# Label logits by masked sums on VectorE in place of 63 of 64 gathers, a tapered last group and one activation table set, in a softmax cross-entropy kernel

## The chip, the cores and the metric

The kernel runs on one core of one Trainium2 chip. The metric is device time in microseconds (us) of one execution. The profile's own span of an execution is 1.3 to 2 us shorter than the time reported for it, so differences inside a run are told in span, and verdicts in time.

Engines: ScalarE (ACT) computes the exponentials, VectorE (DVE) small reductions, GpSimd (POOL) issues the gathers, SyncE (SP) issues the loads, and 16 DMA engines move the data between HBM, the main memory, and SBUF, the on-chip memory. PSUM is a second on-chip memory. A load "lands" when all its data has arrived. `L85` is line 85 of the kernel in question, so the same statement has other line numbers in other kernels.

## The reference

```python
logits: float32 [16, 512, 32000]      # 8192 rows, 1.05 GB
labels: int32   [16, 512]
lse  = log(sum(exp(logits - max))) + max          # per row
loss = lse - logits[row, label[row]]              # float32 [16, 512]
```

Every logit must be read once. That is 1048.6 MB. The kernels leave out the maximum; with the drawn inputs this stays within tolerance.

## The kernel before

The 8192 rows stand as 128 partitions times G = 64 groups. A group has V = 32000 columns.

```python
idx[p, g] = (p * G + g) * V + label[p, g]         # GpSimd: iota, add
for g in range(G):                                # 64 gathers, 128 elements of 4 bytes each
    nc.gpsimd.indirect_dma_start(out=lab_logit[:, g:g + 1], in_=lg,
        in_offset=bass.IndirectOffsetOnAxis(ap=idx[:, g:g + 1], axis=1), ...)
...
for g in range(G):
    if g >= G - FINE_GROUPS:                      # last 3 groups: 8 tiles of 4000 columns each, 5 buffers
        for c in range(CF):
            tf = fine_pool.tile([P, WF], FP32)
            nc.sync.dma_start(out=tf[:], in_=lg_pg[:, g, c * WF:(c + 1) * WF])
            nc.scalar.activation(out=tf[:], in_=tf[:], func=Exp, accum_out=stats_col(g, c))
    else:                                         # 61 groups: 2 tiles of 16000 columns each, 2 buffers
        for c in range(C):
            t = data_pool.tile([P, W], FP32)
            nc.sync.dma_start(out=t[:], in_=lg_pg[:, g, c * W:(c + 1) * W])
            nc.scalar.activation(out=t[:], in_=t[:], func=Exp, accum_out=stats_col(g, c))
...
def finalize(lo, hi):   # sum of the stats (VectorE), Ln (ScalarE), subtract (VectorE), store
    ...
finalize(0, G - 1)
finalize(G - 1, G)
```

The exp is in place: only its row sum (`accum_out`) is of use. One buffer is free again when its exp is over.

The softmax here doesn't subtract the row's maximum and nothing guards it: scores larger than these inputs give would overflow.

## Time and profile before

| | before |
|---|---|
| time, median of 4 runs | 2440.01 us (2439.93 to 2440.22) |
| span of the profiled run | 2438.7 us |
| a 16000-column tile (8.19 MB) lands every | 18.90 us undisturbed, about 19.3 us while the gathers run |
| exp of a 16000-column tile | 13.54 us |
| last logits land | 2430.76 us |
| from there to the end | 7.9 us |

Lines of the page of the kernel before follow. First come the busy time of each engine, then the share of DMA busy time and the GB/s in 40 equal slices of the span. Then come the queue that fetches instructions (packets, MB, share), two groups of instructions (busy us, mean ns, idle time before them and who ended it), and the issues of the large loads (KB each, us from issue to landing).

```profile
span 2438.7 us, 851 instructions
...
DVE 1.7 (0%) x5; ACT 1754.4 (72%) x298; POOL 61.2 (3%) x70
...
DMA  9999999999999999999999999999999999999998
GB/s 404 437 420 422 435 437 435 429 429 437 437 436 428 431 435 437 435 432 428 435 436 436 435 427 434 436 437 435 427 432 436 437 435 425 434 437 432 426 430 360
...
q14 instruction: 6, 0.05, 0.0%
...
L85 ACT ACTIVATE t<-t 128x16000 f32<-128x16000 f32 x122 | 1651.4, 13536 | 642.9 <-DMA t<-in_logits_dram 642.9
...
L57 POOL DMA_INDIRECT lab_logit<-in_logits_dram,idx x64 | 60.5, 945 | 186.8 <-DMA lab_logit<-in_logits_dram,idx 184.2
...
t<-in_logits_dram SPq DMA_DIRECT2D x122, 8000.0 KB, 24.1
```

The load stream bounds this kernel. ScalarE is busy 72% of the time and had 642.9 us of idle time that ended with a landing. The DMA engines are above 90% in nearly every slice. 8.192 MB every 18.90 us is 433 GB/s.

The end of the timeline of the same kernel follows (start us, duration us, engine, line, operation, idle time before it and who ended it).

```profile
2430.84 3.54 ACT L76 ACTIVATE tf<-tf 128x4000 f32<-128x4000 f32 x1 [1.11 <-DMA tf<-in_logits_dram]
...
2434.49 1.28 ACT L101 ACT_TABLE_LOAD   x1
2434.50 0.16 DVE L96 TENSOR_REDUCE totals<-stats_last 128x1 f32<-128x8 f32 x1 [36.37 <-ACT tf L76]
2435.78 0.20 ACT L101 ACTIVATE logsum<-totals 128x1 f32<-128x1 f32 x1
2436.02 0.16 DVE L105 TENSOR_TENSOR res<-logsum,lab_logit 128x1 f32<-128x1 f32 x1 [1.35 <-ACT logsum L101]
2436.21 0.34 ACTq L109 DMA_DIRECT2D out_dram<-res  x1
```

The last of the 4000-column pieces has just landed at 2430.76. Then come an exp of 3.54 us, a table load of 1.28 us (in this trace one stands wherever ScalarE goes from Exp to Ln, at 2396.32 and 2434.49, and from Ln back to Exp, at 2398.62), Ln, subtract and store.

### The profile page before, as it was taken

The page shows a single profiled execution, that of the slowest core. Times are in us where ns is not written, and L with a number is a line of the kernel's source. Part 1 is how long each engine was busy: PE and PEld are TensorE (multiplying, and loading weights), DVE is VectorE, ACT ScalarE, POOL GpSimd, SP SyncE. Part 2 cuts the span into 40 slices and gives each one's busy share as a digit, 9 for nine tenths or more (in the row PEclk, how much of TensorE's full clock was granted, in tenths as well). Part 3 has the DMA queues.
Part 4 walks back from the last instruction along what each step waited for, and adds up shares of the span by engine and source line. Part 5 has one row for each costly group of instructions (what it writes and reads, how often), then busy time and mean ns, then how long its engine had stood idle before and what let it go on. Part 6 is the DMA issues. An engine that isn't in the chain of part 4 may idle for free.

```text
span 2438.7 us, 851 instructions
## 1 busy us (share of the span) xinstructions
DVE 1.7 (0%) x5; ACT 1754.4 (72%) x298; POOL 61.2 (3%) x70
## 2 busy tenths in 40 slices
DVE  0000000000000000000000000000000000000000
ACT  4777766777677767777677767777677767777697
POOL 3222000000000000000000000000000000000000
DMA  9999999999999999999999999999999999999998
GB/s 404 437 420 422 435 437 435 429 429 437 437 436 428 431 435 437 435 432 428 435 436 436 435 427 434 436 437 435 427 432 436 437 435 425 434 437 432 426 430 360
DMA packets 23510, 1048.77 MB, mean 430 GB/s; under 512 B 4688, under 2 KB 4816, under 8 KB 4816
## 3 DMA queue, kind: packets, MB, share of 16 engines
q1 hardware_dynamic: 21168, 1048.65, 99.6%
q0 software_dynamic: 2048, 0.04, 0.1%
q10 hardware_dynamic: 288, 0.03, 0.0%
q14 instruction: 6, 0.05, 0.0%
HBM read 1048.67 MB, written 0.03 MB: 430 GB/s over the span
## 4 chain that ended last, share of the span: by engine, by line
DMA 63%; ACT 36%; issue 0%; ACTq 0%; SPq 0%; DVE 0%
DMA t<-in_logits_dram 61%; ACT t L85 34%; DMA tf<-in_logits_dram 2%; ACT tf L76 2%; ACT L101 0%; ACT L76 0%; ACTq L85 0%; ACT logsum L101 0%; SPq L84 0%; DVE res L105 0%; SPq L48 0%; ACTq L109 0%; ACTq L76 0%
## 5 line engine op out<-in xcount | busy, mean ns | idle before, releaser
L85 ACT ACTIVATE t<-t 128x16000 f32<-128x16000 f32 x122 | 1651.4, 13536 | 642.9 <-DMA t<-in_logits_dram 642.9
L76 ACT ACTIVATE tf<-tf 128x4000 f32<-128x4000 f32 x24 | 84.7, 3530 | 14.6 <-DMA tf<-in_logits_dram 14.6
L57 POOL DMA_INDIRECT lab_logit<-in_logits_dram,idx x64 | 60.5, 945 | 186.8 <-DMA lab_logit<-in_logits_dram,idx 184.2
L85 ACT ACTIVATION_READ_ACCUMULATOR t<-t 128x1 f32 x122 | 22.7, 186 | 0.0
L85 ACT ACT_TABLE_LOAD x1 | 1.3, 1283 | 23.3 <-DMA t<-in_logits_dram 23.3
L76 ACT ACTIVATION_READ_ACCUMULATOR tf<-tf 128x1 f32 x24 | 4.5, 187 | 0.0
L101 ACT ACT_TABLE_LOAD x2 | 2.6, 1283 | 0.0
L96 DVE TENSOR_REDUCE totals<-stats 128x63 f32<-128x504 f32 x1 | 0.7, 678 | 2394.9 <-ACT tf L76 2394.9
L76 ACT ACT_TABLE_LOAD x1 | 1.3, 1283 | 0.8 <-DVE res L105 0.8
L66 DVE MEMSET stats<- 128x504 f32 x1 | 0.5, 478 | 0.9 <-PEq L127 0.9
L101 ACT ACTIVATE logsum<-totals 128x63 f32<-128x63 f32 (+1 forms) x2 | 0.5, 229 | 0.0
L105 DVE TENSOR_TENSOR res<-logsum,lab_logit 128x63 f32<-128x63 f32 (+1 forms) x2 | 0.4, 192 | 2.2 <-ACT logsum L101 2.2
L53 POOL TENSOR_TENSOR idx<-idx,labs 128x64 int32<-128x64 int32 x1 | 0.3, 318 | 1.8 <-DMA labs<-in_labels_dram 1.8
L96 DVE TENSOR_REDUCE totals<-stats_last 128x1 f32<-128x8 f32 x1 | 0.2, 161 | 36.4 <-ACT tf L76 36.4
L51 POOL IOTA idx<- 128x64 int32 x1 | 0.2, 172 | 0.4 <-PEq L138 0.4
L127 POOL MEMSET const-uint8-127<- 128x1 uint8 x1 | 0.1, 118 | 0.0
L127 POOL MEMSET const-bfloat16-1.0<- 128x1 bf16 x1 | 0.1, 113 | 0.0
L127 POOL MEMSET const-float32-0.0<- 128x1 f32 x1 | 0.1, 98 | 0.2 <-issue 0.2
L127 POOL MEMSET const-float32-1.0<- 128x1 f32 x1 | 0.1, 104 | 0.0
## 6 DMA issues: line engine op xcount, KB each, us to landing
t<-in_logits_dram SPq DMA_DIRECT2D x122, 8000.0 KB, 24.1
tf<-in_logits_dram SPq DMA_DIRECT2D x24, 2000.0 KB, 20.1
lab_logit<-in_logits_dram,idx POOLq DMA_INDIRECT x64, 33.4
labs<-in_labels_dram SPq DMA_DIRECT2D x1, 64.0 KB, 1.9
out_dram<-res ACTq DMA_DIRECT2D x1, 31.5 KB, 9.1
out_dram<-res ACTq DMA_DIRECT2D x1, 0.5 KB, 1.4
```

What stands on the lines that cost most here:

```text
L51: nc.gpsimd.iota(idx[:], pattern=[[V, G]], base=0, channel_multiplier=G * V)
L53: nc.gpsimd.tensor_tensor(out=idx[:], in0=idx[:], in1=labs32, op=mybir.AluOpType.add)
L57: nc.gpsimd.indirect_dma_start(out=lab_logit[:, g:g + 1], out_offset=None, in_=lg, in_offset=bass.IndirectOffsetOnAxis(ap=idx[:, g:g + 1], ...
L66: nc.vector.memset(stats[:], 0.0)
L76: nc.scalar.activation(out=tf[:], in_=tf[:], func=mybir.ActivationFunctionType.Exp, accum_out=stats_col(g, c),)
L85: nc.scalar.activation(out=t[:], in_=t[:], func=mybir.ActivationFunctionType.Exp, accum_out=stats_col(g, c),)
L96: nc.vector.reduce_sum(out=totals[:, lo:hi], in_=stats[:, lo:hi, :] if hi <= G - 1 else stats_last[:], axis=mybir.AxisListType.X,)
L101: nc.scalar.activation(out=logsum[:, lo:hi], in_=totals[:, lo:hi], func=mybir.ActivationFunctionType.Ln,)
L105: nc.vector.tensor_tensor(out=res[:, lo:hi], in0=logsum[:, lo:hi], in1=lab_logit[:, lo:hi], op=mybir.AluOpType.subtract,)
L127: nc = _bacc.Bacc("TRN2", target_bir_lowering=False, num_devices=1)
```

## The change

The intent is to take the 64 gathers off the DMA engines, by reading the label logits out of the tiles that are in SBUF anyway, and to shorten the end. For each quarter tile of 4000 columns one VectorE instruction computes `(column == label) * logit` and its row sum, which is the label's logit or 0. Only the last group still uses a gather. Now there are three buffers of 16000 columns. The last group comes in seven shrinking pieces. One table set that holds Exp and Ln is loaded once, at the start (the only table load in the trace of the changed kernel: 1.28 us, from 1.18 us on).

```diff
-    data_pool = ctx.enter_context(tc.tile_pool(name="data", bufs=2))
-    fine_pool = ctx.enter_context(tc.tile_pool(name="fine", bufs=5))
+    data = ctx.enter_context(tc.tile_pool(name="data", bufs=3))
+    masked = psum.tile([P, H], FP32)                            # H = 4000, never read
+    TAPER = [11200, 8000, 5600, 3500, 2000, 1100, 600]
...
-    nc.sync.dma_start(out=labs64[:], in_=labels_pg)
+    nc.scalar.dma_start(out=labs64[:], in_=labels_pg)
+    nc.scalar.preload_act_table_set("natural_log_exp_and_others")
...
-    for g in range(G):
-        nc.gpsimd.indirect_dma_start(out=lab_logit[:, g:g + 1], ...)
+    nc.gpsimd.indirect_dma_start(out=lab_logit[:, G - 1:G], ...)   # last group alone
...
+    for g in range(G - 1):
+        for c in range(C):
+            t = data.tile([P, W], FP32, tag="t")
+            nc.sync.dma_start(out=t[:], in_=lg_pg[:, g, c * W:(c + 1) * W])
+            for i in range(W // H):
+                h = c * (W // H) + i
+                nc.vector.scalar_tensor_tensor(
+                    out=masked[:], in0=cols[:], scalar=lab_at[:, h, g:g + 1],
+                    in1=t[:, i * H:(i + 1) * H],
+                    op0=ALU.is_equal, op1=ALU.mult,
+                    accum_out=found[:, g, h:h + 1])
+            nc.scalar.activation(out=t[:], in_=t[:], func=EXP, accum_out=sums[:, g, c:c + 1])
...
+    for i, n in enumerate(TAPER):                               # pieces share the three buffers
+        nc.sync.dma_start(out=place[i], in_=lg_pg[:, G - 1, starts[i]:starts[i] + n])
+    for i, n in enumerate(TAPER):
+        nc.scalar.activation(out=place[i], in_=place[i], func=EXP, accum_out=sums_last[:, i:i + 1])
```

Because the exp overwrites the tile, it must now wait for the four masked sums of that tile.

More of the change, by code (lines that the diff above doesn't have):

```diff
@@ L7 @@
 from concourse._compat import with_exitstack
+from concourse.masks import make_identity
 FP32 = mybir.dt.float32
 I32 = mybir.dt.int32
+EXP = mybir.ActivationFunctionType.Exp
+LN = mybir.ActivationFunctionType.Ln
+ALU = mybir.AluOpType
 @with_exitstack
@@ L23 @@
     B, S, V = logits.shape
-    N = B * S
     P = 128
-    G = N // P
-    assert N % P == 0
+    G = B * S // P
     W = 16000
     C = V // W
-    assert V % W == 0
-    WF = 4000
-    CF = V // WF
-    FINE_GROUPS = 3
-    assert V % WF == 0
+    H = W // 4
+    NH = V // H
     lg = logits.rearrange("b s v -> (b s) v")
@@ L41 @@
     out_pg = out.rearrange("b s -> (b s)").rearrange("(p g) -> p g", g=G)
-    data_pool = ctx.enter_context(tc.tile_pool(name="data", bufs=2))
-    fine_pool = ctx.enter_context(tc.tile_pool(name="fine", bufs=5))
+    data = ctx.enter_context(tc.tile_pool(name="data", bufs=3))
     persist = ctx.enter_context(tc.tile_pool(name="persist", bufs=1))
+    psum = ctx.enter_context(tc.tile_pool(name="psum", bufs=1, space=bass.MemoryType.PSUM))
+    masked = psum.tile([P, H], FP32)
+    TAPER = [11200, 8000, 5600, 3500, 2000, 1100, 600]
@@ L47 @@
+    assert sum(TAPER) == V
+    NT = len(TAPER)
     labs64 = persist.tile([P, G], mybir.dt.int64)
-    nc.sync.dma_start(out=labs64[:], in_=labels_pg)
-    idx = persist.tile([P, G], I32)
-    nc.gpsimd.iota(idx[:], pattern=[[V, G]], base=0, channel_multiplier=G * V)
+    nc.scalar.dma_start(out=labs64[:], in_=labels_pg)
+    nc.scalar.preload_act_table_set("natural_log_exp_and_others")
     labs32 = labs64[:].bitcast(I32).rearrange("p (g two) -> p g two", two=2)[:, :, 0]
-    nc.gpsimd.tensor_tensor(out=idx[:], in0=idx[:], in1=labs32, op=mybir.AluOpType.add)
@@ L55 @@
-    lab_logit = persist.tile([P, G], FP32)
-    for g in range(G):
-        nc.gpsimd.indirect_dma_start(
-            out=lab_logit[:, g:g + 1],
-            out_offset=None,
-            in_=lg,
-            in_offset=bass.IndirectOffsetOnAxis(ap=idx[:, g:g + 1], axis=1),
-        )
-    stats = persist.tile([P, G - 1, CF], FP32)
-    stats_last = persist.tile([P, 1, CF], FP32)
-    nc.vector.memset(stats[:], 0.0)
-    def stats_col(g, c):
-        return stats[:, g, c:c + 1] if g < G - 1 else stats_last[:, 0, c:c + 1]
@@ L71 @@
-    for g in range(G):
-        if g >= G - FINE_GROUPS:
-            for c in range(CF):
-                tf = fine_pool.tile([P, WF], FP32)
-                nc.sync.dma_start(out=tf[:], in_=lg_pg[:, g, c * WF:(c + 1) * WF])
-                nc.scalar.activation(
-                    out=tf[:], in_=tf[:],
-                    func=mybir.ActivationFunctionType.Exp,
-                    accum_out=stats_col(g, c),
-                )
-        else:
-            for c in range(C):
-                t = data_pool.tile([P, W], FP32)
-                nc.sync.dma_start(out=t[:], in_=lg_pg[:, g, c * W:(c + 1) * W])
-                nc.scalar.activation(
-                    out=t[:], in_=t[:],
-                    func=mybir.ActivationFunctionType.Exp,
-                    accum_out=stats_col(g, c),
-                )
@@ L91 @@
-    totals = persist.tile([P, G], FP32)
-    logsum = persist.tile([P, G], FP32)
-    res = persist.tile([P, G], FP32)
-    def finalize(lo, hi):
-        nc.vector.reduce_sum(
-            out=totals[:, lo:hi],
-            in_=stats[:, lo:hi, :] if hi <= G - 1 else stats_last[:],
-            axis=mybir.AxisListType.X,
-        )
-        nc.scalar.activation(
-            out=logsum[:, lo:hi], in_=totals[:, lo:hi],
-            func=mybir.ActivationFunctionType.Ln,
-        )
-        nc.vector.tensor_tensor(
-            out=res[:, lo:hi], in0=logsum[:, lo:hi], in1=lab_logit[:, lo:hi],
-            op=mybir.AluOpType.subtract,
-        )
-        nc.scalar.dma_start(out=out_pg[:, lo:hi], in_=res[:, lo:hi])
@@ L111 @@
-    finalize(0, G - 1)
-    finalize(G - 1, G)
+    cols = persist.tile([P, H], mybir.dt.uint16)
+    nc.gpsimd.iota(cols[:], pattern=[[1, H]], base=0, channel_multiplier=0)
+    last = persist.tile([P, 1], I32)
+    nc.gpsimd.iota(last[:], pattern=[[V, 1]], base=(G - 1) * V, channel_multiplier=G * V)
+    nc.gpsimd.tensor_tensor(out=last[:], in0=last[:], in1=labs32[:, G - 1:G], op=ALU.add)
+    lab_at = persist.tile([P, NH, G], FP32)
+    for h in range(NH):
+        nc.vector.tensor_scalar(
+            out=lab_at[:, h, :], in0=labs32, scalar1=float(-h * H), scalar2=None, op0=ALU.add
+        )
@@ new lines @@
+    found = persist.tile([P, G, NH], FP32)
+    lab_logit = persist.tile([P, G], FP32)
+    nc.gpsimd.indirect_dma_start(
+        out=lab_logit[:, G - 1:G],
+        out_offset=None,
+        in_=lg,
+        in_offset=bass.IndirectOffsetOnAxis(ap=last[:, 0:1], axis=1),
+    )
+    sums = persist.tile([P, G, C], FP32)
+    for g in range(G - 1):
[5 more added lines that the diff above has]
+                nc.vector.scalar_tensor_tensor(
+                    out=masked[:],
+                    in0=cols[:],
+                    scalar=lab_at[:, h, g:g + 1],
+                    in1=t[:, i * H:(i + 1) * H],
+                    op0=ALU.is_equal,
+                    op1=ALU.mult,
+                    accum_out=found[:, g, h:h + 1],
+                )
+            nc.scalar.activation(out=t[:], in_=t[:], func=EXP, accum_out=sums[:, g, c:c + 1])
@@ new lines @@
+    sums_last = persist.tile([P, NT], FP32)
+    spaces = [[0, 3, 5], [1, 2, 4], [6]]
+    at = 0
+    starts = []
+    for n in TAPER:
+        starts.append(at)
+        at += n
+    place = {}
+    for s in spaces:
+        t = data.tile([P, W], FP32, tag="t")
+        o = 0
+        for i in s:
+            place[i] = t[:, o:o + TAPER[i]]
+            o += TAPER[i]
+    for i, n in enumerate(TAPER):
+        nc.sync.dma_start(out=place[i], in_=lg_pg[:, G - 1, starts[i]:starts[i] + n])
+    for i, n in enumerate(TAPER):
+        nc.scalar.activation(out=place[i], in_=place[i], func=EXP, accum_out=sums_last[:, i:i + 1])
@@ new lines @@
+    totals = persist.tile([P, G - 1], FP32)
+    logsum = persist.tile([P, G - 1], FP32)
+    res = persist.tile([P, G - 1], FP32)
+    nc.vector.reduce_sum(out=totals[:], in_=sums[:, 0:G - 1, :], axis=mybir.AxisListType.X)
+    nc.vector.reduce_sum(out=lab_logit[:, 0:G - 1], in_=found[:, 0:G - 1, :], axis=mybir.AxisListType.X)
+    nc.scalar.activation(out=logsum[:], in_=totals[:], func=LN)
+    nc.vector.tensor_tensor(out=res[:], in0=logsum[:], in1=lab_logit[:, 0:G - 1], op=ALU.subtract)
+    nc.scalar.dma_start(out=out_pg[:, 0:G - 1], in_=res[:])
@@ L116 @@
+    part = persist.tile([P, 1], FP32)
+    nc.vector.reduce_sum(out=part[:], in_=sums_last[:, 0:NT - 1], axis=mybir.AxisListType.X)
+    logsum_last = persist.tile([P, 1], FP32)
+    res_last = persist.tile([P, 1], FP32)
+    nc.scalar.activation(out=logsum_last[:], in_=sums_last[:, NT - 1:NT], func=LN, bias=part[:])
+    nc.vector.tensor_tensor(out=res_last[:], in0=logsum_last[:], in1=lab_logit[:, G - 1:G], op=ALU.subtract)
+    nc.scalar.dma_start(out=out_pg[:, G - 1:G], in_=res_last[:])
 _INS = ['logits', 'labels']
```

## The prediction

> **What bounds it now.** The load stream. The page shows ScalarE 72% busy, VectorE 0%, the 16 DMA engines in the ninth tenth of every slice, 430 GB/s over the span. In the timeline a 16000-column tile (8.19 MB) lands every 18.90 us in the undisturbed part (433 GB/s) and a 4000-column tile every 4.77 us late in the run; fitted together: 434.7 GB/s plus some 0.05 us per DMA. [...] so depth 3 cannot raise the rate. The wait table has ScalarE idle 643 us on loads: slack. A tile is issued 24.06 us before landing, 5.2 more than its transfer.
>
> **Removed.** While the 64 gathers run (3.6 to 250 us) a tile takes 19.30 us instead of 18.90: about 5 us in all, on the stream, so critical. Three table loads of 1.28 us; only the last is on the final chain. The end: last piece landed 2430.84, then exp 3.54, table load, Ln, subtract and store, finishing 7.9 us later. I expect the last logits byte to land near 2425 to 2427 us rather than 2431.
>
> **Added.** 504 VectorE masked sums over 128x4000. No such op is in the trace; a 128x504 TENSOR_REDUCE took 678 ns[...]. Estimate: 4.17+0.15, plus 0.05 to 0.15 for the accumulator read and the wait on its predecessor (one `masked` buffer): about 4.45 us, 17.8 us per tile, under 18.9. Then the stream still bounds the steady state: release comes 17.8+13.6 = 31.4 us after landing, and three buffers allow some 34.
>
> **Moved, and the catch.** ScalarE's in-place exp must now follow VectorE, so it starts about 17.8 us after landing, not at once: it runs a whole tile behind. The instruction order shows exp of the 11200 piece placed before the last 16000 tile. With T the landing of that tile (estimate 2386): the previous tile's exp ends T+12.4; the 11200 piece lands T+13.2, exp 9.6 until T+22.9; the last tile 13.6 until T+36.5; then 8000 … 600 columns, 17680 ns at 0.834 ns/column plus 0.29 each, until about T+55.5. The last piece has landed by T+38 to 41. So the run ends on ScalarE work, some 15 us after the stream. Ln, subtract and store add about 3.5 us. Span about 2445.5, time about 1.3 us more: **2447 us**, range 2436 to 2464. The backlog gives back the gather and table savings (about 8 us).
>
> **Chances.** Faster by over 2%: 0.01 (needs below 2391; the bytes alone take 2412 at 434.7). Within: 0.87. Slower: 0.12.
>
> **What would show it.** Masked sum 4.3 to 4.6 us; steady landing interval 18.9, also in the first 250 us; ScalarE waiting on VectorE, not DMA; at the end ScalarE without a gap for some 42 us from the 11200 piece on, the last piece landed 14 us before its exp; one table load.
>
> **What would make it wrong.** A masked sum above 4.73 us makes VectorE the bound: 126 x 4 x the excess; 4.81 already passes +2%. [...] A stream stalled on buffer release would add to every tile.

## The result, and the profile after

| | before | after |
|---|---|---|
| time, median of 4 runs each | 2440.01 us | 2453.8 us (2453.32 to 2453.99) |
| span of the profiled run | 2438.7 us | 2451.9 us |
| 126 full tiles' worth of logits landed | 2392.6 us | 2393.7 us |
| last logits landed | 2430.8 us | 2433.7 us |
| last exp over | 2434.5 us | 2448.6 us |

The ratio is 1.0056, with a 95% interval of 1.0042 to 1.0070. A ratio here is the mean time of one kernel's fast runs over that of the other's of the same rounds, so it is not quite the ratio of the medians quoted. The change is slower by about 0.6%, which counts as the same at the 2% level.

Lines of the page of the changed kernel:

```profile
span 2451.9 us, 1858 instructions
...
DVE 2246.2 (92%) x1021; ACT 1747.2 (71%) x269; POOL 9.3 (0%) x8
...
GB/s 419 434 434 434 434 434 434 434 434 433 434 433 428 431 431 432 433 434 433 434 428 428 434 433 434 428 431 434 432 428 433 434 432 431 430 431 433 434 422 264
...
q14 instruction: 14, 0.11, 0.0%
...
L91 DVE SCALAR_TENSOR_TENSOR masked<-cols,lab_at,t 128x4000 f32<-128x4000 uint16 x504 | 2214.5, 4394 | 144.2 <-DMA t<-in_logits_dram 130.8
L100 ACT ACTIVATE t<-t 128x16000 f32<-128x16000 f32 x126 | 1705.8, 13538 | 700.1 <-issue 651.4
L91 DVE DVE_READ_ACCUMULATOR masked<-cols,lab_at,t 128x1 f32 x504 | 71.9, 143 | 0.0
```

A masked sum takes 4394 ns and its accumulator read 143 ns more, partly overlapped. In the timeline they start 4.49 us apart. Four of them are 17.9 us, below the 18.90 us of a tile, so VectorE at 92% is not the bound, and the GB/s row stays near 434 in most slices. The gathers' loss in the first slices is gone: the row starts 419, 434, 434, where the kernel before had 404, 437, 420. But the instruction queue shows 14 packets where it showed 6, and some tiles come late. (The dips of the row to 428 do not show this: they are not in the slices where late tiles stand, and the row of the kernel before has dips to 425.)

The timeline of the changed kernel, VectorE alone, shows one late tile. These are the first masked sums of three tiles in a row; the bracket at the end is how long VectorE waited for the landing.

```profile
932.12 4.39 DVE L91 SCALAR_TENSOR_TENSOR masked<-cols,lab_at,t 128x4000 f32<-128x4000 uint16 x1 [0.98 <-DMA t<-in_logits_dram]
...
951.97 4.39 DVE L91 SCALAR_TENSOR_TENSOR masked<-cols,lab_at,t 128x4000 f32<-128x4000 uint16 x1 [1.94 <-DMA t<-in_logits_dram]
...
970.87 4.39 DVE L91 SCALAR_TENSOR_TENSOR masked<-cols,lab_at,t 128x4000 f32<-128x4000 uint16 x1 [0.98 <-DMA t<-in_logits_dram]
```

The tile of the second line came 19.85 us after its forerunner and the next one 18.90 us after it. The wait is 1.94 us in place of 0.98. Over the run eight tiles are late by that amount, at nearly even distances of 14 tiles.

The end of the timeline of the changed kernel, where a table load is no longer to be seen (`L100` is the exp of a full tile, `L120` of a piece):

```profile
2392.91 13.54 ACT L100 ACTIVATE t<-t 128x16000 f32<-128x16000 f32 x1 [5.28 <-issue]
...
2407.03 9.54 ACT L120 ACTIVATE t<-t 128x11200 f32<-128x11200 f32 x1 [0.49 <-DMA t<-in_logits_dram]
...
2416.57 13.52 ACT L100 ACTIVATE t<-t 128x16000 f32<-128x16000 f32 x1
...
2430.09 6.86 ACT L120 ACTIVATE t<-t 128x8000 f32<-128x8000 f32 x1
...
2436.94 4.86 ACT L120 ACTIVATE t<-t 128x5600 f32<-128x5600 f32 x1
...
2447.85 0.69 ACT L120 ACTIVATE t<-t 128x600 f32<-128x600 f32 x1
...
2448.68 0.28 ACT L136 ACTIVATE logsum_last<-sums_last,part 128x1 f32<-128x1 f32 x1
...
2449.45 0.45 ACTq L138 DMA_DIRECT2D out_dram<-res_last  x1
```

The last full tile landed at 2393.7, but ScalarE began the exp of its forerunner only at 2392.91, when VectorE had let go of it. From 2407.03 to 2448.63 ScalarE has no gap. The last piece landed at 2433.70 and waited 14.15 us for its exp. The store is issued at 2449.45, 15.8 us after all logits have landed.

The longest waits of the changed kernel, from its wait table (who waited for whom, us in total, times, longest):

```profile
ACT t L100 <- issue: 651.4, 122, 6.2
DVE masked L91 <- DMA t<-in_logits_dram: 130.8, 124, 2.0
ACT t L100 <- DVE masked L91: 48.7, 3, 39.0
```

ScalarE hardly waits for a DMA any more (0.5 us, at the first piece); VectorE does, for 130.8 us in all, so VectorE too is ahead of the stream. One side effect: the label load, moved to ScalarE's queue, lands at 22.7 us, behind the first tile, where it had landed at 2.7 us. That did no harm that these traces show, since the masked sums need that tile anyway: the next tiles land 18.9 to 19.0 us apart.

So the loss has two candidates: late tiles in the middle, and ScalarE's backlog at the end.

### The profile page after: what moved, and what is told of

Read it like the earlier page. It is cut to its first block, busy times and chain, and to the rows that moved or that the text cites. A ratio compares the mean times of both kernels' runs of the same rounds, so it can differ in the third digit from the quotient of the medians.

```text
span 2451.9 us, 1858 instructions
## 1 busy us (share of the span) xinstructions
DVE 2246.2 (92%) x1021; ACT 1747.2 (71%) x269; POOL 9.3 (0%) x8
## 2 busy tenths in 40 slices
DMA packets 19630, 1048.80 MB, mean 428 GB/s; under 512 B 2464, under 2 KB 2592, under 8 KB 2976
## 4 chain that ended last, share of the span: by engine, by line
DMA 65%; DVE 32%; issue 2%; ACT 1%; DVEq 0%; SPq 0%; ACTq 0%
DMA t<-in_logits_dram 65%; DVE masked L91 32%; ACT t L120 1%; ACT t L100 0%; DVEq L91 0%; SPq L88 0%; ACT logsum_last L136 0%; DVE res_last L137 0%; ACT logsum L128 0%; ACTq L120 0%
## 5 line engine op out<-in xcount | busy, mean ns | idle before, releaser
L91 DVE SCALAR_TENSOR_TENSOR masked<-cols,lab_at,t 128x4000 f32<-128x4000 uint16 x504 | 2214.5, 4394 | 144.2 <-DMA t<-in_logits_dram 130.8
L100 ACT ACTIVATE t<-t 128x16000 f32<-128x16000 f32 x126 | 1705.8, 13538 | 700.1 <-issue 651.4
L91 DVE DVE_READ_ACCUMULATOR masked<-cols,lab_at,t 128x1 f32 x504 | 71.9, 143 | 0.0
L120 ACT ACTIVATE t<-t 128x11200 f32<-128x11200 f32 (+6 forms) x7 | 28.0, 4000 | 0.5 <-DMA t<-in_logits_dram 0.5
L100 ACT ACTIVATION_READ_ACCUMULATOR t<-t 128x1 f32 x126 | 23.6, 188 | 0.0
L70 DVE TENSOR_SCALAR lab_at<-labs 128x64 f32<-128x64 int32 x8 | 0.9, 191 | 22.7 <-DMA labs<-in_labels_dram 22.7
L126 DVE TENSOR_REDUCE totals<-sums 128x63 f32<-128x126 f32 x1 | 0.3, 284 | 17.8 <-ACT t L100 17.8
L76 POOL DMA_INDIRECT lab_logit<-in_logits_dram,last x1 | 5.3, 5311 | 0.5 <-POOL last L65 0.5
L120 ACT ACTIVATION_READ_ACCUMULATOR t<-t 128x1 f32 x7 | 1.3, 187 | 0.0
```

What stands on the lines that cost most here:

```text
L70: nc.vector.tensor_scalar(out=lab_at[:, h, :], in0=labs32, scalar1=float(-h * H), scalar2=None, op0=ALU.add)
L76: nc.gpsimd.indirect_dma_start(out=lab_logit[:, G - 1:G], out_offset=None, in_=lg, in_offset=bass.IndirectOffsetOnAxis(ap=last[:, 0:1], ax ...
L91: nc.vector.scalar_tensor_tensor(out=masked[:], in0=cols[:], scalar=lab_at[:, h, g:g + 1], in1=t[:, i * H:(i + 1) * H], op0=ALU.is_equal, ...
L100: nc.scalar.activation(out=t[:], in_=t[:], func=EXP, accum_out=sums[:, g, c:c + 1])
L120: nc.scalar.activation(out=place[i], in_=place[i], func=EXP, accum_out=sums_last[:, i:i + 1])
L126: nc.vector.reduce_sum(out=totals[:], in_=sums[:, 0:G - 1, :], axis=mybir.AxisListType.X)
```

## The experiments

Theory A: the end is ScalarE's backlog. It runs one tile behind, because the masked sums stand between the landing and the exp. Theory B: the late tiles come from fetching VectorE's long program over the same DMA engines. Rival C: VectorE's reading of the tiles disturbs the loads or delays the release of buffers.

The narrow runs and the run with neither gathers nor masked sums give wrong results.

### Gathers for the last three groups (e1_tail_gather)

```diff
-            for i in range(W // H):
+            for i in range(W // H if g < G - K else 0):        # K = 3: no masked sum in groups 61 to 63
```
(and three gathers in place of one)

> The changed kernel, but the last three groups get their label logits by gathers, so that the masked sums stop four full tiles before the tapered group and ScalarE can catch up. Theory A (the end is ScalarE's backlog of one tile behind VectorE): last full tile lands at about 2393.5 us as in the changed kernel, the tapered exps now follow their landings, last exp ends about 1 us after the last landing (2431.5 to 2432), span about 2436 instead of 2451.9, time about 2437.5. Rival (the small pieces or the tail order are slow in themselves): the gap between last landing and end of the run stays near 18 us, span stays above 2445.

Measured: correct, 2441.64 us (before in the same rounds 2440.18, ratio 1.0006, interval 0.9992 to 1.0019), span 2439.9. The last full tile landed at 2393.9 as in the changed kernel, the last piece at 2432.06. The end of its timeline (`L102` full tile, `L122` piece):

```profile
2393.96 13.54 ACT L102 ACTIVATE t<-t 128x16000 f32<-128x16000 f32 x1 [3.40 <-DMA t<-in_logits_dram]
...
2408.94 9.54 ACT L122 ACTIVATE t<-t 128x11200 f32<-128x11200 f32 x1 [0.74 <-DVE res L131]
...
2418.47 6.85 ACT L122 ACTIVATE t<-t 128x8000 f32<-128x8000 f32 x1
...
2436.23 0.69 ACT L122 ACTIVATE t<-t 128x600 f32<-128x600 f32 x1
...
2437.56 0.34 ACTq L140 DMA_DIRECT2D out_dram<-res_last  x1
```

The exp of the last full tile starts 0.08 us after its landing, where it waited 22.9 us in the changed kernel. With the stream at the same place, the span is 12.0 us shorter. Theory A holds: masked sums up to the very end cost 12 us. The number was off, though. I expected 2436, and the last exp still ends 5.0 us after the last landing. That is a second, smaller backlog, taken up below.

### The same instructions with hardly any data (e2_narrow)

```diff
-                    out=masked[:], in0=cols[:],
-                    in1=t[:, i * H:(i + 1) * H],
+                    out=masked[:, 0:16], in0=cols[:, 0:16],
+                    in1=t[:, i * H:i * H + 16],                # label logits wrong on purpose
```

> The changed kernel with every masked sum cut to 16 columns: same VectorE instruction count, almost no VectorE data (label logits wrong on purpose). Theory B (the load stream loses 0.95 us each time an 8 KB block of instructions is fetched, about every 14 tiles, because 504 masked sums make a long VectorE program): 7 or 8 tiles still take about 19.85 us instead of 18.90, last full tile lands at 2393 to 2394, span about 2436. Rival C (VectorE reading tiles at full rate while the loads write disturbs the loads, or tiles are released too late): the late tiles vanish, last full tile lands at about 2386, span about 2428.5.

Measured: wrong result; 2442.68 us, span 2440.9 (about 2436 was expected; the second backlog again). The last full tile landed at 2393.45, only 0.26 us earlier than with full masked sums. The same three tiles of its timeline:

```profile
932.36 0.24 DVE L91 SCALAR_TENSOR_TENSOR masked<-cols,lab_at,t 128x16 f32<-128x16 uint16 x1 [17.59 <-DMA t<-in_logits_dram]
...
952.24 0.24 DVE L91 SCALAR_TENSOR_TENSOR masked<-cols,lab_at,t 128x16 f32<-128x16 uint16 x1 [18.57 <-DMA t<-in_logits_dram]
...
971.14 0.24 DVE L91 SCALAR_TENSOR_TENSOR masked<-cols,lab_at,t 128x16 f32<-128x16 uint16 x1 [17.59 <-DMA t<-in_logits_dram]
```

A VectorE instruction is now 0.24 us long, the engine idles nearly all the time, buffers are free early, and still the second tile comes 19.88 us after the first and the third 18.90 us after the second. Eight tiles are late, the same ones. Rival C is refuted: neither the reads nor the release of buffers make them late.

### All gathers, no masked sums (e3_all_gather), and neither (e4_neither)

The first deletes the masked sums from the changed kernel and issues 64 gathers; three buffers, taper and table set stay. The second has one gather alone, so that 63 groups lack their label logit.

```diff
-            for i in range(W // H):
-                nc.vector.scalar_tensor_tensor(...)
+    for k in range(K):                    # K = 64 (e3), K = 1 (e4)
+        nc.gpsimd.indirect_dma_start(out=lab_logit[:, G - K + k:G - K + k + 1], ...)
```

> The changed kernel without the masked sums; all 64 label logits by gathers as before; three buffers, taper and the one table set stay. If A and B hold: no instruction-fetch pattern, but the first 13 tiles take about 19.3 us again (5 us in all), last full tile lands at about 2391, span about 2433.5, time about 2435: faster than both kernels. If the three buffers or the taper do harm of their own: span at or above 2438.7 of before.

> As the run with all gathers, but only one gather and no masked sums (63 of 64 groups get no label logit: wrong on purpose). The floor of the stream. If the costs simply add: last full tile lands at 2385.5 to 2387, span about 2428.5, that is 5 us under the all-gather run and 7.5 us under the narrow run. If gathers cost nothing (rival), it equals the all-gather run within 1 us.

Measured: all gathers, correct, 2439.3 us (ratio 0.9997, interval 0.9983 to 1.0010), span 2437.5, last full tile at 2391.53. Neither: wrong, 2434.36 us, span 2432.6, last full tile at 2386.59, within the expected stretch. The floor of the stream is thus 2386.6; the gathers (64 against one) cost it 4.9 us (2391.53 - 2386.59); the 504 masked-sum instructions cost it 6.9 us (2393.45 - 2386.59), which is more than what they replace. Both spans are about 4 us above what I expected, again at the end: in the all-gather run the last piece landed at 2429.71, and its exp was over at 2434.66. The exp of the last full tile, 0.08 us after its landing, in the run with all gathers and below it in the run with neither:

```profile
2391.61 13.54 ACT L80 ACTIVATE t<-t 128x16000 f32<-128x16000 f32 x1 [5.28 <-DMA t<-in_logits_dram]
```

```profile
2386.67 13.54 ACT L81 ACTIVATE t<-t 128x16000 f32<-128x16000 f32 x1 [5.27 <-DMA t<-in_logits_dram]
```

### Program length as a dose (e5_narrow_twice, e6_narrow_half)

The narrow run with every masked sum issued twice (1008), and with every second one left out (252).

```diff
-            for i in range(W // H):
+            for i in list(range(W // H)) * 2:      # e5
+            for i in range(0, W // H, 2):          # e6
```

> The narrow run with each masked sum issued twice (1008 instead of 504): the VectorE program is twice as long, its data still next to nothing. Theory B (instruction fetches): 15 or 16 tiles of about 19.85 us, one every 7 to 8 tiles, last full tile lands at about 2400 to 2401. Rival (a fixed disturbance every 14 tiles that has nothing to do with program length): 8 late tiles, 2393.5.

> The narrow run with half of the masked sums (252). Theory B: 4 or 5 late tiles, one every 25 or so, last full tile lands at about 2390. Rival: 8 late tiles, 2393.5.

The instruction queue of the doubled run, and below it that of the halved run (packets, MB, share of the engines' span):

```profile
q14 instruction: 22, 0.18, 0.0%
```

```profile
q14 instruction: 10, 0.08, 0.0%
```

With none and with 504 masked sums the queue shows 5 and 14 packets. The first masked sum of the last full tile, about 0.1 us after its landing, in the halved, the narrow and the doubled run:

```profile
2389.74 0.24 DVE L92 SCALAR_TENSOR_TENSOR masked<-cols,lab_at,t 128x16 f32<-128x16 uint16 x1 [18.26 <-DMA t<-in_logits_dram]
```

```profile
2393.55 0.24 DVE L91 SCALAR_TENSOR_TENSOR masked<-cols,lab_at,t 128x16 f32<-128x16 uint16 x1 [17.59 <-DMA t<-in_logits_dram]
```

```profile
2401.37 0.24 DVE L91 SCALAR_TENSOR_TENSOR masked<-cols,lab_at,t 128x16 f32<-128x16 uint16 x1 [16.24 <-DMA t<-in_logits_dram]
```

| masked sums | tiles late by 0.9 us or more | last full tile landed | over the run with none |
|---|---|---|---|
| 0 (e4) | 0 | 2386.59 us | |
| 252 (e6) | 4 | 2389.65 us | 3.1 us |
| 504 (e2) | 8 | 2393.45 us | 6.9 us |
| 1008 (e5) | 16 | 2401.27 us | 14.7 us |

The cost follows the length of the program. In the doubled run late tiles are 7 or 8 tiles apart; in the halved one 25 or 26. (The runs without masked sums have two tiles late by 0.7 us and the halved one has one late by 0.64; an instruction fetch stands at each of these too.) The DMA packet records of the narrow run show how. Each DMA engine moves a tile's rows in packets of 64,000 bytes of 2.37 us. At each of the eight late tiles an instruction packet of 8192 bytes runs for 0.32 to 0.33 us, and the data packet that starts as it ends takes 3.02 us. That is 0.33 + (3.02 - 2.37) = 0.98 us, the delay seen. In the records of the changed kernel the same stands at seven of its eight late tiles: a fetch of 0.32 to 0.33 us and a data packet of 3.02 us behind it. A tile has landed when all its packets have, and no later tile came early to make up for it. The narrow run's delays, eight of 0.94 to 0.98 us and one of 0.61, are 8.3 us; the run without masked sums has 1.6 us of such delays at its own five fetches; the difference of 6.7 us is nearly the whole 6.9. Not every fetch delays a tile (two of those five do not), and why the packet behind a fetch is 0.65 us longer stays open, too.

### One table set alone (e7_one_table)

```diff
+    nc.scalar.preload_act_table_set("natural_log_exp_and_others")   # in the kernel before, nothing else
```

> The kernel before with nothing changed but the one activation table set loaded at the start. Only the last of the three later table loads is on the final chain: span 1.28 us less (2437.4), time about 2438.7. Rival (all three count): 3.8 us less.

Measured: correct, 2439.18 us against 2440.13 of the same rounds (ratio 0.9996, interval 0.9982 to 1.0009), span 2437.2. The end of its timeline (`L77` is the exp, `L102` Ln):

```profile
2430.43 3.54 ACT L77 ACTIVATE tf<-tf 128x4000 f32<-128x4000 f32 x1 [1.12 <-DMA tf<-in_logits_dram]
...
2434.09 0.16 DVE L97 TENSOR_REDUCE totals<-stats_last 128x1 f32<-128x8 f32 x1 [36.94 <-ACT tf L77]
2434.28 0.20 ACT L102 ACTIVATE logsum<-totals 128x1 f32<-128x1 f32 x1 [0.23 <-DVE totals L97]
...
2434.71 0.34 ACTq L110 DMA_DIRECT2D out_dram<-res  x1
```

From the last landing to the end it took 6.9 us (2437.2 - 2430.34), 1.1 less than before. Of the 1.28 us of the table load 0.2 come back: Ln now waits 0.23 us for VectorE's reduction, which the load used to hide. The profiler's inferred chain of the kernel before runs through the other two loads as well (at 2396.32 and 2398.62), but without them nothing is gained there: from 126 tiles' worth to the last landing it took 38.17 us before and 38.16 here. The remaining 0.4 us of the span lie in the stream before that, where spans of one kernel differ by as much. The interval of the ratio does not exclude no gain at all; the timeline shows it.

### An end with which ScalarE keeps up (e8_fine_end)

What held e1, e3 and e4 up by 4 us: behind the landing of the last full tile stand 48000 columns of exp (its own 16000 and the last group). In the all-gather run ScalarE took 43.0 us for it (2391.61 to 2434.66: 13.6 for the tile, 1.3 for the results of the first 63 groups, which come between, 28.1 for the pieces), the stream 38.2 (2391.53 to 2429.71). No division of the last group alone can mend this: 48000 columns at 0.834 ns, the slope between the exps of 16000 and of 4000 columns before, are 40.0 us without any fixed cost. So the last but one group gets smaller tiles too.

```diff
+    TAPER = [4300, 7200, 5300, 4000, 3000, 2400, 1900, 1500, 1300, 1100]
-    for g in range(G - 1):
+    for g in range(G - 2):                # full tiles; the last but one group then comes as 4 pieces of 8000
```

> All gathers, one table set, and an end in which ScalarE can keep up: the last but one group in four pieces of 8000 columns, the last in ten pieces from 7200 down to 1100, each small enough that its exp (0.834 ns per column plus 0.29 us) is over when the next lands. In the all-gather run the last exp ended 5.0 us after the last landing because a 16000-column tile stood right before the taper. If that is the cause: last landing at about 2430, last exp ends 1.3 us later, span about 2434, time 2435.8, against 2440.2 before and 2439.3 for all gathers. Rival (the tail is bound by something other than that tile): span stays at 2437 to 2438.

Measured: correct, 2436.04 us (2435.85 to 2436.20) against 2440.13 in the same rounds, ratio 0.9983, interval 0.9969 to 0.9996; span 2434.4. The last piece landed at 2430.12. The end of its timeline:

```profile
2405.43 6.20 ACT L109 ACTIVATE t<-t 128x7200 f32<-128x7200 f32 x1 [2.83 <-DMA t<-in_logits_dram]
...
2425.39 1.79 ACT L109 ACTIVATE t<-t 128x1900 f32<-128x1900 f32 x1
...
2430.14 1.12 ACT L109 ACTIVATE t<-t 128x1100 f32<-128x1100 f32 x1
...
2431.39 0.29 ACT L124 ACTIVATE logsum_last<-sums_last,part 128x1 f32<-128x1 f32 x1
...
2431.91 0.34 ACTq L126 DMA_DIRECT2D out_dram<-res_last  x1
```

The last exp starts as its piece lands and is over 1.2 us later. This version is faster than both kernels: by 4.1 us than the one before (0.17%, the same at the 2% level), by 17.8 than the changed one (of other rounds). It is the gathers of the old kernel with the three buffers and the one table set of the new one and an end sized anew.

## Why the prediction was right or wrong

The time fell in the range (2436 to 2464), 6.8 us above the central value, and the chances put 0.87 on within 2%. Against the kernel before, a loss of 7 us was forecast and 13.8 were measured. The mechanism of the end was foreseen; a second cost, which the prediction did not have, nearly doubled the loss, and that it still fell in the range is owed to the width of the range. Point by point:

- **The stream bounds, and depth 3 does not raise its rate.** Right. That depth 3 could not raise it was the author's estimate; the runs show that it did not: an undisturbed tile takes 18.90 us with two buffers and with three.
- **A masked sum of about 4.45 us, 17.8 us per tile.** Right: 4.49 and 17.9. The 4.17 + 0.15 of the forecast is what the line through two reductions of the kernel before gives for 4000 columns: 161 ns for 8 columns and 678 ns for 504, so 1.04 ns per column and 0.15 us besides. The subtractions of that kernel, with two sources, took 159 ns for 1 column and 225 ns for 63, 1.06 ns per column. The 0.05 to 0.15 us for the accumulator read and the wait were the author's estimate, which that trace does not show. Measured, with a uint16 and an fp32 source: 4394 ns for 4000 columns against 244 ns for 16 (e2), which is again 1.04 ns per column, and 0.10 us more until the next one starts.
- **Gathers cost the stream about 5 us.** Right: 4.9 us (e3 against e4), for 63 gathers of 128 four-byte elements each, 0.08 us a gather.
- **Of three table loads only the last counts, 1.28 us.** Nearly right: 1.1 us (e7).
- **ScalarE's backlog at the end.** Right, step by step. With T the landing of the last full tile, at 2393.7: exp of the 11200 piece from T+13.3 (predicted T+13.2), the last tile's exp over at T+36.4 (T+36.5), the last exp at T+54.9 (T+55.5), the last piece landed at T+40.0 (T+38 to 41). The gap-free stretch was 41.6 us (42). e1 shows that it costs 12.0 us.
- **"I expect the last logits byte to land near 2425 to 2427 us."** Wrong: 2433.7. This is the step that failed, through its T of 2386, which was 7.7 us early. The estimate had only what the change takes off the stream and nothing that it puts on. The run with neither gathers nor masked sums had its T at 2386.59, where the prediction put it. The runs showed 6.9 us on top for the instructions of the 504 masked sums, which the dose and the packet records put down to their fetching, and 0.3 for their data (2393.72 - 2393.45).
- **"The backlog gives back the gather and table savings (about 8 us)."** Half the story: the instruction fetches alone give back more than the gathers had cost, and the backlog comes on top.
- **ScalarE waiting on VectorE.** Right. The wait table names VectorE for only 48.7 us and puts 651.4 us down to "issue", but in the timeline 124 of the 126 exps start within some 0.1 us of the end of the tile's last masked sum, so these are the same wait.

The sum, in span: the stream at 126 tiles' worth is 1.1 us later. That is 6.87 for the masked sums' instructions and 0.26 for their data, less 4.94 for the gathers, less 1.06 for the rest of the change (e3 against the kernel before; 0.9 of it stands at the first landing already, 22.39 us against 23.27). From there to the end it took 46.1 us before and 58.1 after, 12.0 more. Together 13.1 us, the difference of the spans (2451.86 - 2438.71). In e1 and e3 that last stretch is 46.0 us: taper and table set, freed of the backlog, gained nothing, because the taper still had a full tile in front of it. With that mended (e8) the stretch is 42.7 us.

## What to carry to other kernels

In this kernel, which fills the DMA engines, instructions were traffic too: 504 of them cost the stream 6.9 us and the gathers that they replaced 4.9. So compare the stream with and without the work before moving it from DMA to an idle engine. What the same full work in a shorter program would cost, no run shows. An in-place pass put between landing and the next consumer cost 0.3 us up to the last full tile here, beyond its instructions, and 12.0 us at the end; stop it some tiles early. Size an end taper by the backlog of the last consumer, from the first tile that it cannot finish before the next lands.
